# Four attention scalings moved from GpSimd to ScalarE, and the first weight unit cast by two engines

## The chip, the cores and the metric

The kernel runs on one core of a Trainium2 chip. One core has five engines that work side by side, each through its own list of instructions in a fixed order: TensorE (PE: matrix products, and transposes against an identity), VectorE (DVE), ScalarE (ACT), GpSimd (POOL) and SyncE (SP), which here issues nearly all of the transfers (DMAs). An instruction starts when the one ahead of it on its engine has gone and when the semaphores that it waits for have come. The working memory is SBUF; matrix products are written to PSUM, which has eight banks of 128 x 512 float32. The metric is the time of one execution in device microseconds; lower is better.

## The reference

One decoder layer on 512 tokens of 2048 channels, in float32. The normed input goes through one projection whose columns feed three mixers; their outputs go through one output projection, a residual, a second norm and a SwiGLU.

```python
h = _rms_norm(x, norm1_g[l])
proj = h @ w_in[l]
aq, ak, av, bu, bg, cq, ck, cv = jnp.split(proj, splits, axis=-1)
...
out_a = _dilated_mixture(aq, ak, av)              # 8 heads x 64
out_b = _conformer_conv(bu, bg, ...)              # 512 channels, 31 taps
out_c, _ = _band_attention(cq, ck, cv, 127, sinks=...)   # 16 query heads, 2 key heads
mix = jnp.concatenate([out_a, out_b, out_c], axis=-1)
x = x + mix @ w_out[l]
h2 = _rms_norm(x, norm2_g[l])
x = x + (jax.nn.silu(h2 @ w_gate[l]) * (h2 @ w_up[l])) @ w_down[l]
```

For one head of group A the three dilated patterns are one softmax over all earlier keys in which a key's weight is multiplied by the number of patterns that hold it (0 to 3). So a head needs scores, a masked maximum, exponentials, a product with that number, a sum, and a division by the sum before the values are weighed.

## The kernel before, in words

**Products in three terms.** A float32 product is made of three products of a rounded type: each operand is split into a high part `hi` (a cast, on ScalarE) and a low part `lo` (operand less high part, on VectorE), and `mm3` multiplies high by high, one high by the other low, and low by high. In the first stage the tokens are the operand loaded into the array and the weights the one that streams. All the kernel's rows of 128 x 512 on TensorE are such terms.

**Weights.** `pump` (L277 holds its transfer) loads weight units of up to 128 x 1024 in a fixed order into a few raw buffers. `split_up_to` (L289 the cast on ScalarE, L290 the subtraction on VectorE) makes `wh` and `wl` of a unit, two units ahead of the products that use it; there are three buffers of each.

**Opening.** For tile `k` of the 16 tiles of 128 channels, `scaled` makes the high part of the normed input on ScalarE (L419) and the low part on VectorE (L420). Then 12 products (four token tiles `in0` to `in3`, three terms each: L312, L313, L314) are added to four banks. The first two units hold the weights of one tile `k` each (128 x 512). Eight products of zeros (L409) run while the first data come in.

**Projection, attention, output projection.** Later units are taken one after the other (`project`, then `first_two` and a loop for the output projection `o`). Work of the mixers is hung between the products by a table of due times (`Ticks`): TensorE's order is written out by the main loop, and each `ticks.tick()` appends what is due to the lists of all engines. So where an instruction stands in an engine's list is fixed when the program is built, and an instruction that must wait holds up what stands behind it on its engine.

**One head of group A** (`attention`, name `a0` to `a3` for a pair of heads, head 0 or 1 in it). The four query tiles have 128, 256, 384 and 512 keys, in three units: `e..0` (tiles of 128 and 256), `e..1` (384), `e..2` (512: the last query tile). For each unit: `scores` on TensorE into a PSUM bank `s`; `top` on VectorE (L750, L753); `exps` on ScalarE (L763, out of PSUM into an SBUF tile `e`); `norm`: VectorE multiplies by the number of patterns and sums (L775), takes the reciprocal (L777), and GpSimd scales the tile by it (L779). Then `flip` transposes the tiles on TensorE (L795) into a bank `t`, ScalarE and VectorE split that bank (L801 `ph`, L806 `pl`), and `weigh` multiplies by the values (L819, L820) into a bank `o`, which L828 (ScalarE) and L833 (VectorE) put together in `mix`.

**Splitting the mixers' outputs.** `split_mix` casts a tile of the mixed outputs on ScalarE (L864, `mh`) and subtracts on GpSimd for group C or on VectorE for A and B (L865, `ml`). The output projection's first two column tiles (`first_two`) use `mh` and `ml` of rows c0, c1, c2, c4, c5, c3, c7, c6 in this order, six products a row, and they begin while heads `a1` to `a3` are still under way.

**Keys of the pair `a3`** pass over a bank too: `ak3wide` (L622, ScalarE), transposes (L629) into the bank `ak3t`, and two VectorE instructions that read it (L635). PSUM banks go round: the second transposes of head 1 of `a1` write the bank that `ak3t` had, and `aq3f` (L568) the one that the scores of 384 keys of `a2` had.

Of the kernel before, what the change touches and what calls it, by code (L numbers as in the profile page):

```python
# [9 lines left out]
F32 = mybir.dt.float32  # L10
F32R = mybir.dt.float32r
I32 = mybir.dt.int32
AF = mybir.ActivationFunctionType
ALU = mybir.AluOpType

P = 128
T = 512
NT = T // P
D = 2048
KT = D // P  # L20
# [67 lines left out]
C_G1, C_G2, C_CW, C_CB, C_LG, C_LB, C_QK, C_SINK, C_ALL = 0, 16, 32, 156, 160, 164, 168, 172, 188  # L88
# [34 lines left out]
def kernel(ctx: ExitStack, tc: tile.TileContext, xT, wi, wo, wgu, wd, cst_in, outT):  # L123
    nc = tc.nc
# [33 lines left out]
    units = [wi[0][:, :T], wi[0][:, T:]] + [wi[u] for u in range(1, 2 * N_IN)]  # L158
# [7 lines left out]
    raws, held = {}, {}  # L166
# [101 lines left out]
    splits = {}  # L268
# [11 lines left out]
    def split_up_to(i):  # L280
        while at["split"] <= min(i, len(works) - 1):
            key, last, eng = works[at["split"]]
            t, n = drop(key) if last else raws[key]
            u = at["split"]
            hi = wp.tile([P, 1024], F32R, name=f"wh{u}", tag="hi", bufs=SPLIT_BUFS)
            lo = wp.tile([P, 1024], F32R, name=f"wl{u}", tag="lo", bufs=SPLIT_BUFS)
            if eng or u < len(units) + 4:
                eng = eng or nc.vector
                nc.scalar.copy(hi[:, :n], t[:, :n])  # L289
                eng.tensor_sub(lo[:, :n], t[:, :n], hi[:, :n].bitcast(F32))  # L290
            else:
                near = psum["high"].tile([P, 1024], F32R, name=f"wn{u}", tag="h")
                nc.scalar.copy(near[:, :n], t[:, :n])
                nc.scalar.copy(hi[:, :n], t[:, :n])
                nc.vector.tensor_sub(lo[:, :n], t[:, :n], near[:, :n].bitcast(F32))  # L295
            splits[u] = (hi, lo)
            at["split"] += 1
# [13 lines left out]
    def mm3(out, wh, wl, xh, xl, start, stop):  # L311
        nc.tensor.matmul(out, wh, xh, start=start, stop=False)  # L312
        nc.tensor.matmul(out, wh, xl, start=False, stop=False)  # L313
        nc.tensor.matmul(out, wl, xh, start=False, stop=stop)  # L314
# [4 lines left out]
    xs = []  # L319
# [6 lines left out]
    for k in range(X_AHEAD):  # L326
        load_first(k)
        u = k if k < 2 else k // 2 + 1
# [18 lines left out]
    def col(i):  # L347
        return cst[:, i:i + 1]
# [64 lines left out]
    def scaled(x, g, tag, k):  # L413
        if k < N_WIDE:
            both = wide(k, f"{tag}{k}", F32R)
            hi, lo = both[:, :T], both[:, T:]
        else:
            hi, lo = slot(f"{tag}h{k}", F32R), slot(f"{tag}l{k}", F32R)
        nc.scalar.activation(hi, x, AF.Copy, scale=g)  # L419
        nc.vector.scalar_tensor_tensor(lo, x, g, hi.bitcast(F32), op0=ALU.mult, op1=ALU.subtract)  # L420
        return hi, lo
# [19 lines left out]

    g4 = [(column if j < COLUMN_BANKS - 1 else bank)(f"in{j}") for j in range(HEAD4)]
    h_hl = {}
    for k in range(2):
        h_hl[k] = scaled(xs[k], col(C_G1 + k), "h", k)
        split_up_to(k)
    pump(RAW_EARLY)
    add_square(ssum, xs[0], 0, "sq")
    for k in range(KT):
        if k + 2 < KT:  # L450
            h_hl[k + 2] = scaled(xs[k + 2], col(C_G1 + k + 2), "h", k + 2)
        if k < 2 or k % 2 == 0:
            wh, wl = next_unit()
            o = 0
        if k + X_AHEAD < KT:
            load_first(k + X_AHEAD)
        if k == 4:
            nc.sync.dma_start(cst[:, C_G2:], cst_in[:, C_G2:])
        if k + 1 < KT:
            add_square(ssum, xs[k + 1], k + 1, "sq")  # L460
        hi, lo = h_hl.pop(k)
        h_hi.append(hi)
        h_lo.append(lo)
        for i in range(NT):
            s = slice(i * P, (i + 1) * P)
            mm3(g4[i], hi[:, s], lo[:, s], wh[:, o:o + T], wl[:, o:o + T], k == 0, k == KT - 1)
        o += T
    xs = None
    c64 = cp.tile([P, NT], F32, name="c64")
# [245 lines left out]
    def attention(kind, box, mix, mi, heads):  # L715
        ready, every, step, s1, sx, s2, fl, ev, we = C_TICKS if kind == "c" else A_TICKS
        name = mi
# [5 lines left out]
        def head(h):  # L723
            es = {}
            d = cp.tile([P, 4, NT], F32, name=f"{name}d{h}", tag="soft", bufs=6)
            mx, nm, den, rd = (d[:, i] for i in range(4))
# [41 lines left out]
            def norm(u):  # L768
                e = es[u]
                s = slice(us[u][0][0], us[u][-1][0] + 1)  # L770
                if kind == "c":
                    nc.vector.tensor_add(den[:, s], den[:, s], mx[:, s])
                else:
                    for i, k0, n, o in us[u]:
                        nc.vector.scalar_tensor_tensor(e[:, o:o + n], e[:, o:o + n], 1.0, mult_a[:, T - n:],  # L775
                                                       op0=ALU.mult, op1=ALU.mult, accum_out=den[:, i:i + 1])
                nc.vector.reciprocal(rd[:, s], den[:, s])  # L777
                for i, k0, n, o in us[u]:
                    nc.gpsimd.tensor_scalar(e[:, o:o + n], e[:, o:o + n], rd[:, i:i + 1], None, op0=ALU.mult)  # L779

            ph, pl = {}, {}

# [57 lines left out]
            t0 = max(ticks.now + ready, head_at[0], box["q at"] - s1, box["k at"], box["v at"] - at_v)  # L840
# [37 lines left out]
    g4 = b = None  # L878
# [151 lines left out]
    for half in range(2):  # L1030
        for i, n in enumerate(OUT_ORDER[half]):
# [9 lines left out]
            wh, wl = next_unit()  # L1041
            if half == 1 and i == KT - 1:
                drop(first_sum[0][1])
            for kk in range(8):
                if half == 1 and i == KT - 2 and kk == 4:
                    first_sum[0][0]()
                k = 8 * half + kk
# [4 lines left out]
                s = slice(kk * P, (kk + 1) * P)  # L1052
# [345 lines left out]
    for g in range(2 * NP + N_DOWN):  # L1398
        t = g - 2 * NP
# [136 lines left out]
```

## Time and profile before

| | |
|---|---|
| median of 3 runs | 1879.7 us (1879.08 to 1879.79) |
| the profiled execution | 1879.36 us; its span, first to last instruction, 1877.5 us |
| TensorE clock granted | 1.000 |
| busy: PE, DVE, ACT, POOL | 1871.7, 1454.1, 1343.7, 1217.0 us |
| the chain of work that ended last | 96% PE, 1% each DVE, ACT, POOL and issue |
| 397 to 414 us: busy PE, DVE, ACT, POOL | 16.44, 15.50, 12.74, 16.19 of 17.00 us |

Rows of the timeline give start, duration, engine, line, operation and tiles, and in brackets how long the engine was idle just before and what ended that. Matrix products overlap: the duration of a row is longer than the step from its start to the next start, and a wait shows as a longer step. Vector and scalar instructions overlap too, by about a tenth of a microsecond. PEld is the load of the stationary operand, which runs ahead of its product.

### The profile page before, as it was taken

The page shows a single profiled execution, that of the slowest core. Times are in us where ns is not written, and L with a number is a line of the kernel's source. Part 1 is how long each engine was busy: PE and PEld are TensorE (multiplying, and loading weights), DVE is VectorE, ACT ScalarE, POOL GpSimd, SP SyncE. Part 2 cuts the span into 40 slices and gives each one's busy share as a digit, 9 for nine tenths or more (in the row PEclk, how much of TensorE's full clock was granted, in tenths as well). Part 3 has the DMA queues.
Part 4 walks back from the last instruction along what each step waited for, and adds up shares of the span by engine and source line. Part 5 has one row for each costly group of instructions (what it writes and reads, how often), then busy time and mean ns, then how long its engine had stood idle before and what let it go on. Part 6 is the DMA issues. An engine that isn't in the chain of part 4 may idle for free.

```text
span 1877.5 us, 28557 instructions
## 1 busy us (share of the span) xinstructions
PE 1871.7 (100%) x9848; PEld 1609.1 (86%) x9848; DVE 1454.1 (77%) x2376; ACT 1343.7 (72%) x1883; POOL 1217.0 (65%) x812
## 2 busy tenths in 40 slices
PE   9999999999999999999999999999999999999999
PEld 7888888888888888888888888888888888888888
DVE  7578999897679777777777777777777677778887
ACT  6246655553466887888878888888888887777675
POOL 5023444362155887778878877888787767766786
PEclk9999999999999999999999999999999999999999
DMA  7333233333342354443544445344455475578984
GB/s 271 122 109 102 81 105 102 121 107 138 113 146 89 114 178 142 163 163 132 184 134 164 162 137 181 132 166 160 145 175 196 151 237 185 196 253 283 311 241 124
DMA packets 157986, 301.09 MB, mean 160 GB/s; under 512 B 29968, under 2 KB 69008, under 8 KB 157840
## 3 DMA queue, kind: packets, MB, share of 16 engines
q1 hardware_dynamic: 157696, 299.25, 48.8%
q8 instruction: 78, 1.28, 0.3%
q14 instruction: 68, 0.56, 0.1%
q10 hardware_dynamic: 144, 0.01, 0.0%
HBM read 241.27 MB, written 50.33 MB: 155 GB/s over the span
## 4 chain that ended last, share of the span: by engine, by line
PE 96%; DVE 1%; issue 1%; ACT 1%; POOL 1%; DMA 0%; SPq 0%; DVEq 0%; POOLq 0%; ACTq 0%
PE out L1125 51%; PE out L1267 16%; PE o L313 3%; PE o L314 3%; PE o L312 3%; PE cq L312 1%; PE cq L313 1%; PE cq L314 1%; PE in L313 1%; PE ak L312 1%; PE bg L312 1%; PE ak L314 1%; PE ak L313 1%; PE bu L312 1%; PE bu L314 1%; PE bg L313 1%
## 5 line engine op out<-in xcount | busy, mean ns | idle before, releaser
L1125 PE MATMUL out<-h,wh 128*128 128x512 f32 x2464 | 588.4, 391 | 0.0
L1125 PEld LDWEIGHTS out<-h,wh 128*128 128x128 f32 x2464 | 452.7, 188 | 87.5
L1125 PEld LDWEIGHTS out<-h,wl 128*128 128x128 f32 x2464 | 316.2, 191 | 12.4 <-DVE wl L295 0.4
L1125 PE MATMUL out<-h,wl 128*128 128x256 f32 x2464 | 320.3, 283 | 0.2 <-DVE wl L295 0.2
L1267 PE MATMUL out<-wh,a 128*128 128x512 f32 x896 | 221.3, 389 | 0.0
L1267 PEld LDWEIGHTS out<-wh,a 128*128 128x128 f32 x896 | 168.2, 188 | 34.9
L289 ACT CAST wh<-w 128x1024 fp32r<-128x1024 f32 (+1 forms) x93 | 96.7, 1042 | 125.0 <-PE o L313 43.3
L290 DVE TENSOR_TENSOR wl<-w,wh 128x1024 fp32r<-128x1024 f32 (+1 forms) x93 | 117.2, 1262 | 46.7 <-ACT wh L289 45.7
L1267 PE MATMUL out<-wl,a 128*128 128x512 f32 x448 | 119.7, 389 | 0.0
L1267 PEld LDWEIGHTS out<-wl,a 128*128 128x128 f32 x448 | 84.1, 188 | 17.4
L513 DVE SCALAR_TENSOR_TENSOR y<-bu,cst,y 128x511 f32<-128x511 f32 (+14 forms) x120 | 90.3, 753 | 0.7
L1125 PE MATMUL out<-a,wh 128*128 128x512 f32 x330 | 80.1, 391 | 0.0
L1125 PEld LDWEIGHTS out<-a,wh 128*128 128x128 f32 x330 | 60.2, 188 | 11.4
L312 PE MATMUL o<-mh_c,wh 128*128 128x512 f32 x128 | 51.2, 400 | 0.0
L313 PE MATMUL o<-ml_c,wh 128*128 128x512 f32 x128 | 50.1, 392 | 0.4 <-POOL ml_c L865 0.3
L314 PE MATMUL o<-mh_c,wl 128*128 128x512 f32 x128 | 50.1, 391 | 0.0
L1312 DVE TENSOR_TENSOR Y<-Y,out 128x512 f32<-128x512 f32 x48 | 30.8, 683 | 19.0 <-PE out L1267 18.9
L1125 PEld LDWEIGHTS out<-a,wl 128*128 128x128 f32 x330 | 43.3, 191 | 2.2
L1125 PE MATMUL out<-a,wl 128*128 128x256 f32 x330 | 44.0, 283 | 0.0
L429 POOL TENSOR_TENSOR ssum<-ssum,sq 128x512 f32<-128x512 f32 x15 | 26.6, 1770 | 19.3 <-ACT sq L428 18.8
L312 PE MATMUL cq<-hh,wh 128*128 128x512 f32 x96 | 38.6, 402 | 0.0
L314 PE MATMUL cq<-hh,wl 128*128 128x512 f32 x96 | 37.5, 391 | 0.0
(3111 smaller groups left out, 5197.0 us busy)
## 6 DMA issues: line engine op xcount, KB each, us to landing
od<-a SPq DMA_DIRECT2D x140, 256.0 KB, 4.7
a<-od SPq DMA_DIRECT2D x140, 256.0 KB, 6.2
w<-in_wi SPq DMA_DIRECT2D x59, 512.0 KB, 3.6
w<-in_wo SPq DMA_DIRECT2D x32, 512.0 KB, 3.6
x<-in_xT SPq DMA_DIRECT2D x16, 256.0 KB, 6.7
xr<-in_xT SPq DMA_DIRECT2D x16, 256.0 KB, 3.8
x2d<-xr SPq DMA_DIRECT2D x16, 256.0 KB, 2.0
yd<-z SPq DMA_DIRECT2D x16, 256.0 KB, 5.5
```

The source lines that it names most:

```text
L289: nc.scalar.copy(hi[:, :n], t[:, :n])
L290: eng.tensor_sub(lo[:, :n], t[:, :n], hi[:, :n].bitcast(F32))
L312: nc.tensor.matmul(out, wh, xh, start=start, stop=False)
L313: nc.tensor.matmul(out, wh, xl, start=False, stop=False)
L314: nc.tensor.matmul(out, wl, xh, start=False, stop=stop)
L429: eng.tensor_add(acc, acc, sq)
L513: nc.vector.scalar_tensor_tensor(yconv[j][:, i:], hconv[j][:, :T - i], c, yconv[j][:, i:], op0=ALU.mult, op1=ALU.add)
L1125: nc.tensor.matmul(out, lhs[:, s], rhs, start=begin, stop=last and low == flip[0] and x is xs[-1], skip_group_check=True)
L1267: nc.tensor.matmul(to[h], x[:, h * P:(h + 1) * P], v[:, j], start=sub == 0 and h not in started, stop=sub == 1 and n in (len(todo) - 1, le ...
L1312: nc.vector.tensor_add(t, t, b)
```

## The change

There are two parts. They touch no transfer's order and no product's operands.

*Last query tiles of `a1` and `a2`.* In `norm`, the tile of 512 keys of both heads of `a1` and of `a2` is scaled by ScalarE (an activation that copies with a scale per partition) and no longer by GpSimd: four instructions. The order of the lists follows: the instruction now stands in ScalarE's list where GpSimd's stood in time.

*First weight unit.* VectorE casts the first 128 columns of unit 0 and ScalarE the other 384 (before: ScalarE all 512); the first tile's 12 products go term by term over the four token tiles: high x high four times, low tokens x high weights four times, high tokens x low weights four times.

```diff
+            if u == 0:
+                nc.vector.tensor_copy(hi[:, :P], t[:, :P])
+            elif eng or u < len(units) + 4:
...
-    for k in range(2):
-        h_hl[k] = scaled(xs[k], col(C_G1 + k), "h", k)
-        split_up_to(k)
+    t0 = raws[0][0]
+    split_up_to(0)
+    h_hl[0] = scaled(xs[0], col(C_G1), "h", 0)
+    hi, lo = splits[0]
+    nc.scalar.copy(hi[:, P:T], t0[:, P:T])
+    nc.vector.tensor_sub(lo[:, :T], t0[:, :T], hi[:, :T].bitcast(F32))
+    t0 = None
+    h_hl[1] = scaled(xs[1], col(C_G1 + 1), "h", 1)
+    split_up_to(1)
...
+        if k == 0:
+            for x, w in ((hi, wh), (lo, wh), (hi, wl)):
+                for i in range(NT):
+                    nc.tensor.matmul(g4[i], x[:, i * P:(i + 1) * P], w[:, :T], start=x is hi and w is wh, stop=False)
+            continue
...
-                    nc.gpsimd.tensor_scalar(e[:, o:o + n], e[:, o:o + n], rd[:, i:i + 1], None, op0=ALU.mult)
+                    if name in ("a1", "a2") and i == 3:
+                        nc.scalar.activation(e[:, o:o + n], e[:, o:o + n], AF.Copy, scale=rd[:, i:i + 1])
+                    else:
+                        nc.gpsimd.tensor_scalar(e[:, o:o + n], e[:, o:o + n], rd[:, i:i + 1], None, op0=ALU.mult)
```

TensorE's list at the opening, first tile, before. `in0` to `in3` are the four banks, `wh0` and `wl0` the halves of unit 0; the tile named `h0` holds both the high and the low part of the input (L314 reads the low one).

```order
L312 MATMUL in0_139<-wh0_146,h0_143 128x512
L313 MATMUL in0_139<-wl0_147,h0_143 128x512
L314 MATMUL in0_139<-wh0_146,h0_143 128x512
L312 MATMUL in1_140<-wh0_146,h0_143 128x512
L313 MATMUL in1_140<-wl0_147,h0_143 128x512
L314 MATMUL in1_140<-wh0_146,h0_143 128x512
L312 MATMUL in2_141<-wh0_146,h0_143 128x512
L313 MATMUL in2_141<-wl0_147,h0_143 128x512
```

The same place on TensorE in the changed kernel, the first nine:

```order
L475 MATMUL in0_139<-wh0_143,h0_146 128x512
L475 MATMUL in1_140<-wh0_143,h0_146 128x512
L475 MATMUL in2_141<-wh0_143,h0_146 128x512
L475 MATMUL in3_142<-wh0_143,h0_146 128x512
L475 MATMUL in0_139<-wh0_143,h0_146 128x512
L475 MATMUL in1_140<-wh0_143,h0_146 128x512
L475 MATMUL in2_141<-wh0_143,h0_146 128x512
L475 MATMUL in3_142<-wh0_143,h0_146 128x512
L475 MATMUL in0_139<-wl0_144,h0_146 128x512
```

The first product that reads `wl0` stood second and stands ninth. The second tile's products are in the old order in both.

ScalarE's list where head 1 of `a1` ends, before. `a1e12` is the tile of 512 keys of head 1, `wh63` the high half of a weight unit, `mh_c2` and `mh_c4` high parts of rows c2 and c4.

```order
L763 ACTIVATE a1e12_4064<-a1s12_3975,a1d1_3612,aq1r_3746 128x512
L801 CAST a1ph02_4069<-a1t02_4036 128x256
L563 COPY aq3raw_4089<-aq3_3938 128x512
L289 CAST wh63_4119<-w63_3545 128x1024
L864 CAST mh_c2_4126<-mix_c2_2446 128x512
L622 COPY ak3wide_4138<-ak3r_4073 128x512
L864 CAST mh_c4_4140<-mix_c4_3088 128x512
L763 ACTIVATE a2e00_4159<-a2s00_4042,a2d0_3780,aq2r_3921 128x128
```

The same place on ScalarE in the changed kernel (lines are moved by 13 to 16):

```order
L776 ACTIVATE a1e12_4065<-a1s12_3976,a1d1_3613,aq1r_3747 128x512
L817 CAST a1ph02_4070<-a1t02_4037 128x256
L793 ACTIVATE a1e12_4065<-a1e12_4065,a1d1_3613 128x512
L576 COPY aq3raw_4090<-aq3_3939 128x512
L291 CAST wh63_4120<-w63_3546 128x1024
L880 CAST mh_c2_4127<-mix_c2_2447 128x512
L635 COPY ak3wide_4139<-ak3r_4074 128x512
L880 CAST mh_c4_4141<-mix_c4_3089 128x512
```

The new row L793 stands ahead of the copy, the weight cast and the casts of the mixed rows; all else keeps its order.

GpSimd's list at the same place, before and then changed; `ml_c2`, `ml_c4` and `ml_c5` are low parts of mixed rows.

```order
L585 TENSOR_TENSOR ak3r_4073<-ak3v_4055,nhalf_106 128x8
L779 TENSOR_SCALAR a1e12_4064<-a1e12_4064,a1d1_3612 128x512
L865 TENSOR_TENSOR ml_c2_4127<-mix_c2_2446,mh_c2_4126 128x512
L865 TENSOR_TENSOR ml_c4_4141<-mix_c4_3088,mh_c4_4140 128x512
L865 TENSOR_TENSOR ml_c5_4173<-mix_c5_2209,mh_c5_4172 128x512
```

And GpSimd in the changed kernel:

```order
L598 TENSOR_TENSOR ak3r_4074<-ak3v_4056,nhalf_106 128x8
L881 TENSOR_TENSOR ml_c2_4128<-mix_c2_2447,mh_c2_4127 128x512
L881 TENSOR_TENSOR ml_c4_4142<-mix_c4_3089,mh_c4_4141 128x512
L881 TENSOR_TENSOR ml_c5_4174<-mix_c5_2210,mh_c5_4173 128x512
L795 TENSOR_SCALAR a2e00_4160<-a2e00_4160,a2d0_3781 128x128
```

The scaling of `a1e12` is gone from this list, so that `ml_c2` follows `ak3r` directly.

More of the change, by code (lines that the diff above doesn't have):

```diff
@@ L286, in split_up_to @@
             lo = wp.tile([P, 1024], F32R, name=f"wl{u}", tag="lo", bufs=SPLIT_BUFS)
-            if eng or u < len(units) + 4:
+            if u == 0:
+                nc.vector.tensor_copy(hi[:, :P], t[:, :P])
+            elif eng or u < len(units) + 4:
                 eng = eng or nc.vector
@@ L463 @@
         h_lo.append(lo)
+        if k == 0:
[3 more added lines that the diff above has]
+            continue
         for i in range(NT):
             s = slice(i * P, (i + 1) * P)
-            mm3(g4[i], hi[:, s], lo[:, s], wh[:, o:o + T], wl[:, o:o + T], k == 0, k == KT - 1)
+            mm3(g4[i], hi[:, s], lo[:, s], wh[:, o:o + T], wl[:, o:o + T], False, k == KT - 1)
         o += T
```

## The prediction

> **What bounds the kernel now.** The page comes first: in the table, TensorE is busy 1871.7 us of a span of 1877.5 us, and the chain that ended last is 96% TensorE. So only what TensorE waits for can be won, and only what newly makes it wait can be lost. I read next who TensorE's loads of the stationary operand waited for over the whole span (total us, times, longest). These are the rows that the change can touch:
>
> ```profile
> PEld o L313 <- POOL ml_c L865: 1.1, 2, 0.7
> PEld in L313 <- DVE wl L290: 1.1, 3, 0.5
> ...
> PEld a1t L795 <- PE o L314: 0.5, 1, 0.5
> ```
>
> The first row is low parts that come late from GpSimd, the second low halves of weights in the opening, the third transposes of head 1 of `a1`. The row names TensorE itself for the third; of the transposes' two conditions (their bank read out, and the product before them), the bank is meant, as shown below. Together they are 2.7 us, 0.14% of the time, and a load's wait is partly covered by the product before it. I therefore take the losses from TensorE's own steps, from start to start. The step of undisturbed products is 405.95 - 405.73 = 0.22 to 0.23 us in the second set of rows below.
>
> **The opening.** The timeline, TensorE, ScalarE and VectorE in turn:
>
> ```profile
> 5.26 0.50 PE L312 MATMUL in<-wh,h 128*128 128x512 f32 x1
> 5.99 0.50 PE L313 MATMUL in<-wl,h 128*128 128x512 f32 x1 [0.23 <-DVE wl L290]
> ...
> 8.88 0.47 PE L313 MATMUL in<-wl,h 128*128 128x512 f32 x1
> ...
> 11.76 0.50 PE L313 MATMUL in<-wl,h 128*128 128x512 f32 x1
> ...
> 4.59 0.62 ACT L289 CAST wh<-w 128x512 fp32r<-128x512 f32 x1
> 6.67 0.73 ACT L419 ACTIVATE h<-x,cst 128x512 fp32r<-128x512 f32 x1 [1.46 <-DMA x<-in_xT]
> 7.45 0.62 ACT L289 CAST wh<-w 128x512 fp32r<-128x512 f32 x1
> ...
> 9.40 1.05 ACT L289 CAST wh<-w 128x1024 fp32r<-128x1024 f32 x1 [0.18 <-DMA w<-in_wi]
> ...
> 5.24 0.69 DVE L290 TENSOR_TENSOR wl<-w,wh 128x512 fp32r<-128x512 f32 x1
> ...
> 8.11 0.69 DVE L290 TENSOR_TENSOR wl<-w,wh 128x512 fp32r<-128x512 f32 x1
> ...
> 10.48 1.22 DVE L290 TENSOR_TENSOR wl<-w,wh 128x1024 fp32r<-128x1024 f32 x1 [0.48 <-ACT wh L289]
> ```
>
> The second product stands 0.73 us behind the first where 0.23 would do: 0.50 us lost to `wl0` (5.24 + 0.69 = 5.93). In the changed kernel ScalarE casts 384 of the 512 columns, 0.62 x 3/4 = 0.47 us (0.62 if length did not matter), so the first product starts 0 to 0.15 us earlier, at 5.11 to 5.26. VectorE's cast of 128 columns has no row; a quarter of the 0.69 of L290 is 0.17, and the whole 0.69 bounds it (nothing at the other end). It moves `wl0` to 6.1, at worst 6.6. That is needed only by the ninth product, at 5.11 + 8 x 0.23 = 6.95, so the cast is hidden. The first tile's twelve products then end at about 7.9 to 8.0, some 0.7 us earlier than before.
>
> That does not last. The second product of the next tile reads `wl1`, which VectorE ends at 8.11 + 0.69 = 8.80, from ScalarE's cast at 7.45, which stands behind the activation at 6.67, which waited for a transfer of x. None of these moves. So this product starts at 8.88 as before, and the 0.7 us become idle time ahead of it. The next tile has the same end: `wl2` is there at 10.48 + 1.22 = 11.70, its cast at 9.40 waited for a transfer, and its product starts at 11.76 as before. The opening's term is 0, with -0.1 to +0.1 for edges. If the cover is gone (x and weights landing 0.7 us earlier) it would be -0.5.
>
> **Three losses at 402 to 413 us.** TensorE's rows:
>
> ```profile
> 402.46 0.47 PE L312 MATMUL o<-mh_c,wh 128*128 128x512 f32 x1
> 403.07 0.50 PE L313 MATMUL o<-ml_c,wh 128*128 128x512 f32 x1
> ...
> 405.73 0.39 PE L313 MATMUL o<-ml_c,wh 128*128 128x512 f32 x1
> 405.95 0.39 PE L314 MATMUL o<-mh_c,wl 128*128 128x512 f32 x1
> 406.48 0.63 PE L795 MATMUL a1t<-ident,a1e 128*128 128x128 f32 x4
> ...
> 412.56 0.40 PE L312 MATMUL o<-mh_c,wh 128*128 128x512 f32 x1
> 413.25 0.50 PE L313 MATMUL o<-ml_c,wh 128*128 128x512 f32 x1 [0.28 <-POOL ml_c L865]
> ```
>
> L313 at 403.07 and at 413.25 read `ml` tiles: (0.61 - 0.23) + (0.69 - 0.23) = 0.38 + 0.46 us lost. The transposes at 406.48 follow by 0.53 instead of 0.23: 0.30 us. The sum, 1.14 us, is all that freeing GpSimd can give back. Now the other engines at that place:
>
> ```profile
> 397.50 0.59 ACT L563 COPY aq3raw<-aq 128x512 f32<-128x512 f32 x1 [2.68 <-PE aq L314]
> 397.98 1.05 ACT L289 CAST wh<-w 128x1024 fp32r<-128x1024 f32 x1
> 398.93 0.62 ACT L864 CAST mh_c<-mix_c 128x512 fp32r<-128x512 f32 x1
> ...
> 400.49 0.91 ACT L763 ACTIVATE a2e<-a2s,a2d,aq2r 128x128 f32<-128x128 f32 x2
> ...
> 407.14 0.59 ACT L801 CAST a1ph<-a1t 128x512 fp32r<-128x512 f32 x1 [1.04 <-PE a1t L795]
> ...
> 398.68 0.16 DVE L777 RECIPROCAL a1d<-a1d 128x1 f32<-128x1 f32 x1
> ...
> 399.08 1.22 DVE L290 TENSOR_TENSOR wl<-w,wh 128x1024 fp32r<-128x1024 f32 x1
> ...
> 400.87 0.16 DVE L753 SCALAR_TENSOR_TENSOR a2d<-a2d,aq2r 128x1 f32<-128x1 f32 x1
> ...
> 403.10 1.19 DVE L753 SCALAR_TENSOR_TENSOR a2d<-a2d,aq2r 128x1 f32<-128x1 f32 x1
> ...
> 404.81 1.52 DVE L635 SCALAR_TENSOR_TENSOR ak<-ak3raw,gqk,ak3t 64x512 f32<-64x512 f32 x2
> ...
> 399.04 2.62 POOL L779 TENSOR_SCALAR a1e<-a1e,a1d 128x512 f32<-128x512 f32 x1
> 401.63 4.43 POOL L865 TENSOR_TENSOR ml_c<-mix_c,mh_c 128x512 fp32r<-128x512 f32 x3
> ```
>
> *What GpSimd's row removes.* The scaling of head 1's last tile, 2.62 us at 399.04, stands ahead of three `ml` at 401.63. Without it GpSimd would be free for `ml_c2` at 399.04.
>
> *What ScalarE's row adds.* The new instruction stands ahead of the copy at 397.50, but it needs the reciprocal, which VectorE ends at 398.68 + 0.16 = 398.84. ScalarE, in order, must wait until about 398.88. The instruction's own price: same form as L419 (copy with a scale per partition, 512 columns), 0.73 us at 6.67; a row overlaps its follower by 0.59 - 0.48 = 0.11, so 0.62 of the engine. (Ends: 0.5, a plain copy's step, and 0.73.) The copy starts at 399.50 instead of 397.50, and all behind it is 2.0 us later until ScalarE's next idle time, 1.04 us at 407.14.
>
> *First loss.* `mh_c2` moves from 398.93 to 400.93 and ends, with its 0.62, at 401.55. `ml_c2` on GpSimd can start then: at 401.63, where it started before. GpSimd's list is free earlier, but its input comes exactly so much later. The 0.38 us stay: term 0, -0.1 to +0.1.
>
> *Second loss.* VectorE's `wl63` at 399.08 now waits for ScalarE's cast, 397.98 + 2.0 + 1.05 = 401.03: 1.95 us late. What stands behind it on VectorE (the maximum and the products of `a2`, fed by exponentials that slip from 400.49 to 402.5, then the pair L635 at 404.81) slips by some 1.75 us (0.2 us allowed for the gaps between its rows). L635 reads the bank `ak3t` and ended at 404.81 + 1.52 = 406.33; the load for the transposes into that bank followed at once, their row at 406.48. So TensorE waits for VectorE here. How late L635 is now hangs on one row: L753 at 403.10 took 1.19 us for one column, though the same form took 0.16 at 400.87. It ended just when a GpSimd `ml` did (three in 4.43 us from 401.63, the second to about 404.4). If it runs free this time, VectorE gets 1.03 of the 1.75 back and TensorE's wait grows by 0.7; if the third `ml` holds it (404.85 to about 405.8), by 1.65.
>
> The Trainium skill, "SBUF — State Buffer", section "Who interferes with whom", says that a VectorE instruction with two SBUF inputs and a GpSimd one that reads SBUF exclude each other for the whole instruction, and that who issues second waits. The row of 1.19 us agrees; the one of 0.16 us ran while GpSimd's scaling was under way, and does not. By that rule the sum would be at its upper end, by the row of 0.16 at its lower one.
>
> *Third loss.* GpSimd starts its `ml` row at 401.63 as before and does the same work after it, so the last `ml` is still there at about 413.2. TensorE, 0.7 to 1.65 us late, comes after that: the 0.46 us are no longer lost. Net at 413 us: 0.7 - 0.46 = +0.24 to 1.65 - 0.46 = +1.19. I take the middle, +0.7, since neither of the two L753 rows is nearer.
>
> *The other three moved scalings* fall where ScalarE idled:
>
> ```profile
> 389.76 1.05 ACT L289 CAST wh<-w 128x1024 fp32r<-128x1024 f32 x1 [3.68 <-PE aq L313]
> ...
> 413.78 2.00 ACT L289 CAST wh<-w 128x1024 fp32r<-128x1024 f32 x2 [2.54 <-PE o L313]
> ...
> 434.29 1.05 ACT L289 CAST wh<-w 128x1024 fp32r<-128x1024 f32 x1 [4.18 <-PE o L313]
> ...
> 387.49 1.91 POOL L779 TENSOR_SCALAR a1e<-a1e,a1d 128x512 f32<-128x512 f32 x1 [1.77 <-PE aq L313]
> ...
> 414.80 2.37 POOL L779 TENSOR_SCALAR a2e<-a2e,a2d 128x512 f32<-128x512 f32 x1 [1.60 <-DVE a2d L777]
> ...
> 434.76 1.57 POOL L779 TENSOR_SCALAR a2e<-a2e,a2d 128x512 f32<-128x512 f32 x1 [5.01 <-DVE a2d L777]
> ```
>
> Head 0 of `a1`: the reciprocal is there by 387.49; with 0.62 and the two exponentials now behind it (0.91 at 400.49) ScalarE is done by 389.1, before its next row at 389.76. Head 0 of `a2`: ready by 414.80, so the weight casts of 413.78 slip by 414.80 + 0.62 - 413.78 = 1.6. Head 1: 434.76 + 0.62 - 434.29 = 1.1. Those casts are for units two ahead, and a unit is 24 products x 0.23 = 5.5 us of TensorE, which hides both; without that cover they would cost 1.6 + 1.1. GpSimd's 1.91, 2.37 and 1.57 us there come back as idle time. TensorE does not wait again in this stage, so what it is late at 413 us it carries to the end.
>
> **Sum.** Against the profiled execution: 1879.36 + 0 (opening) + 0.7 = 1880.1. The median of the three runs lies 0.34 us above that execution, so I say 1880.2, between 1880.1 and 1879.7 + 0.7.
>
> **The rivals.** A: GpSimd's relief gets through. If the reciprocal came some 2 us earlier, ScalarE would not wait, `ml_c2` would start by 400 and the three losses go: 1879.36 - 1.14 = 1878.2, and 1877.7 if the opening's 0.5 is kept too. For it: GpSimd is 16.19 of 17.00 us busy there (table) and holds VectorE up at least once. Against it: the reciprocal's row stands behind VectorE work that the change leaves alone.
>
> B: the opposite side, one mechanism: ScalarE's wait is passed on in full. It decides at the pair L635. If it ends later than about 406.8, the change costs time; to be over 0.2% slower it must end at 410.5 or later (3.8 + 0.46 us). The terms at hand, 1.95 with no slack taken, two `ml` holds of 1.4 and 1.0, give 406.33 + 4.3 = 410.7 and the time 1879.36 + 4.3 - 0.46 = 1883.2. No single row speaks for so much.
>
> C: the opening does what it says and no more comes of the rest: 1879.36 - 0.5 = 1878.9. The transfers at 6.67 and 9.40 speak against it.
>
> **How the numbers follow.** Forecast (+0.2 to +1.2) 0.62; A 0.22; C 0.10; B 0.04; something not seen, faster by over 0.2%, 0.02. About 0.2%, 3.8 us, is what a measurement of this kernel can tell from no change; the forecast, A and C all lie inside. So faster 0.02, same 0.93, slower 0.05 (B, and a little of the forecast's tail). The forecast alone spans 1879.5 to 1880.9 with the offset of the median. The range takes in A's near end and some way towards B: 1878.0 to 1881.5.
>
> **What would show it.** Opening: first product near 5.1, twelve steps of 0.23 without a hole, then a hole ahead of the product of `wl1`, still at about 8.9, and that of `wl2` at 11.8. Attention: ScalarE idle ahead of the new row until about 398.9, the copy near 399.5, `wl63` near 401.0, `ml_c2` near 401.6, the transposes after L635 at 407.2 to 408.2, no hole ahead of the last `ml`. The prediction is wrong if TensorE reaches 414 us earlier than before, or if a new wait of over 1 us stands anywhere after 440 us.

## The result, and the profile after

The changed kernel takes 1882.09 us (median of 20 runs, 1881.56 to 1882.57) against 1879.44 us before (20 runs, 1878.83 to 1879.91): ratio 1.0014, 95% interval 1.0008 to 1.002. It is 2.65 us slower, and the whole interval lies above 1. That is under the 0.2% that the forecast named as its bound for "the same", but the time lies above the forecast range of 1878.0 to 1881.5. The granted clock is 1.00, as before. The profiled execution took 1882.12 us. In the experiments below a few executions of most kernels, of the kernel before too, took 1.3 to 2.2 us longer than the others at the same clock, so that the highest times stand far from the medians.

Its page, first the span and the totals, then the chain that ended last:

```profile
span 1880.3 us, 28551 instructions
...
PE 1872.0 (100%) x9848; PEld 1609.1 (86%) x9848; DVE 1457.1 (77%) x2377; ACT 1345.6 (72%) x1887; POOL 1209.0 (64%) x808
...
PE 96%; DVE 3%; ACT 1%; issue 0%; DMA 0%; SPq 0%; DVEq 0%
```

TensorE's work is the same (1871.7 us before); the span is 2.8 us longer, so the loss is idle time. What TensorE waited for in the changed kernel (total us, times, longest):

```profile
PE a1t L811 <- DVE ak L648: 1.7, 1, 1.7
...
PE a1t L811 <- DVE mix_a L849: 1.1, 1, 1.1
PE o L315 <- POOL ml_c L881: 0.5, 1, 0.5
```

Two waits are new: the second and the third transposes of head 1 of `a1` (L811, L795 before) wait for VectorE, 1.7 us for the pair that reads the bank `ak3t` (L648, L635 before) and 1.1 us for `mix_a` (L849, L833 before). The busy times of the stretch that the table of before shows (PE, PEld, DVE, ACT and POOL, each with its count):

```profile
397.00:414.00 17.00, 13.76 (x72) 10.83 (x71) 14.68 (x33) 13.12 (x25) 12.66 (x11) 1.00 0.43 114
```

GpSimd is 3.5 us less busy there (16.19 before), 2.62 us of it by the scaling that has left its list, and TensorE does 2.7 us less in the same stretch (16.44 before). The rows of the stretch, ScalarE, VectorE, GpSimd and TensorE in turn:

```profile
398.89 0.72 ACT L793 ACTIVATE a1e<-a1e,a1d 128x512 f32<-128x512 f32 x1 [4.12 <-DVE a1d L790]
399.52 0.57 ACT L576 COPY aq3raw<-aq 128x512 f32<-128x512 f32 x1
399.98 1.05 ACT L291 CAST wh<-w 128x1024 fp32r<-128x1024 f32 x1
400.94 0.61 ACT L880 CAST mh_c<-mix_c 128x512 fp32r<-128x512 f32 x1
...
401.06 1.23 DVE L292 TENSOR_TENSOR wl<-w,wh 128x1024 fp32r<-128x1024 f32 x1 [1.89 <-ACT wh L291]
...
403.58 1.51 DVE L788 SCALAR_TENSOR_TENSOR a2e<-a2e,mult_a 128x256 f32<-128x256 f32 x1
...
405.98 0.27 DVE L766 SCALAR_TENSOR_TENSOR a2d<-a2d,aq2r 128x1 f32<-128x1 f32 x1
...
406.78 1.52 DVE L648 SCALAR_TENSOR_TENSOR ak<-ak3raw,gqk,ak3t 64x512 f32<-64x512 f32 x2
408.33 2.87 DVE L687 TENSOR_TENSOR av<-av3s,av 128x256 fp32r<-128x256 f32 x2
411.23 0.68 DVE L849 TENSOR_TENSOR mix_a<-mix_a,a1o 64x512 f32<-64x512 f32 x1
...
401.63 4.61 POOL L881 TENSOR_TENSOR ml_c<-mix_c,mh_c 128x512 fp32r<-128x512 f32 x3 [2.57 <-ACT mh_c L880]
406.22 2.02 POOL L795 TENSOR_SCALAR a2e<-a2e,a2d 128x128 f32<-128x128 f32 x2
408.20 2.71 POOL L881 TENSOR_TENSOR ml_c<-mix_c,mh_c 128x512 fp32r<-128x512 f32 x2
...
402.53 0.47 PE L314 MATMUL o<-mh_c,wh 128*128 128x512 f32 x1
403.48 0.50 PE L315 MATMUL o<-ml_c,wh 128*128 128x512 f32 x1 [0.47 <-POOL ml_c L881]
...
406.34 0.40 PE L316 MATMUL o<-mh_c,wl 128*128 128x512 f32 x1
408.44 0.63 PE L811 MATMUL a1t<-ident,a1e 128*128 128x128 f32 x4 [1.71 <-DVE ak L648]
...
410.51 0.40 PE L316 MATMUL o<-mh_c,wl 128*128 128x512 f32 x1
411.96 0.44 PE L811 MATMUL a1t<-ident,a1e 128*128 128x128 f32 x2 [1.06 <-DVE mix_a L849]
...
415.77 0.40 PE L314 MATMUL o<-mh_c,wh 128*128 128x512 f32 x1
416.00 0.39 PE L315 MATMUL o<-ml_c,wh 128*128 128x512 f32 x1
```

And the rows of the kernel before that answer to them and that the prediction did not show:

```profile
401.44 0.43 DVE L775 SCALAR_TENSOR_TENSOR a2e<-a2e,mult_a 128x256 f32<-128x256 f32 x1 [0.16 <-ACT a2e L763]
...
406.36 0.76 DVE L674 TENSOR_TENSOR av<-av3s,av 128x256 fp32r<-128x256 f32 x2
407.15 0.68 DVE L833 TENSOR_TENSOR mix_a<-mix_a,a1o 64x512 f32<-64x512 f32 x1
...
406.05 1.79 POOL L779 TENSOR_SCALAR a2e<-a2e,a2d 128x128 f32<-128x128 f32 x2
407.80 2.92 POOL L865 TENSOR_TENSOR ml_c<-mix_c,mh_c 128x512 fp32r<-128x512 f32 x2
...
408.54 0.39 PE L314 MATMUL o<-mh_c,wl 128*128 128x512 f32 x1
408.77 0.38 PE L795 MATMUL a1t<-ident,a1e 128*128 128x128 f32 x2
```

Read the two sets side by side. ScalarE's copy is 2.02 us later (397.50 to 399.52), and VectorE's list from `wl63` on with it (399.08 to 401.06): the `av` pair, two subtractions that make the low part of a3's values, goes from 406.36 to 408.33. GpSimd's list hardly moves: its two `ml` (rows c3 and c7) go from 407.80 to 408.20. Before, the pair ran beside GpSimd's two scalings and took 0.76 us. Now it starts just behind GpSimd's `ml`, takes 2.87 us, and ends 0.3 us behind them (411.2 and 410.9). `mix_a` behind it is there 4.08 us later.

TensorE's losses, below called its holes, each a step less the 0.23 us of an undisturbed one:

| at | before | after | difference |
|---|---|---|---|
| `ml_c2` | 0.38 | 403.48 - 402.53 - 0.23 = 0.72 | +0.34 |
| transposes after `ak3t` | 0.30 | 408.44 - 406.34 - 0.23 = 1.87 | +1.57 |
| transposes after `mix_a` | 408.77 - 408.54 - 0.23 = 0 | 411.96 - 410.51 - 0.23 = 1.22 | +1.22 |
| last `ml` | 0.46 | 416.00 - 415.77 - 0.23 = 0 | -0.46 |

The sum is +2.67 us. TensorE came 0.07 us later to the first of them (402.46 before, 402.53 now), and the last product stands 416.00 - 413.25 = 2.75 us later. The medians differ by 2.65.

The opening, TensorE, ScalarE and VectorE:

```profile
5.37 2.40 PE L475 MATMUL in<-wh,h 128*128 128x512 f32 x8
...
8.91 0.50 PE L315 MATMUL in<-wl,h 128*128 128x512 f32 x1
...
11.80 0.41 PE L315 MATMUL in<-wl,h 128*128 128x512 f32 x1
...
4.80 0.51 ACT L450 CAST wh<-w 128x384 fp32r<-128x384 f32 x1 [0.44 <-DMA w<-in_wi]
...
4.80 0.23 DVE L288 CAST wh<-w 128x128 fp32r<-128x128 f32 x1 [3.15 <-DMA w<-in_wi]
```

The products of `wl1` and `wl2` start at 8.91 and 11.80 (8.88 and 11.76 before), whatever the first tile does. And the first tile itself gains little: the product behind its twelve starts at 8.51 against 8.66 before, since the weights came late and the first two steps took 0.60 and 0.28 us (products at 5.37, 5.96 and 6.24). Why these steps are that long, no run shows.

### The profile page after: what moved, and what is told of

Same layout as the page of the kernel before. It is cut to its first block, busy times and chain, and to the rows that moved or that the text cites. A ratio compares the mean times of both kernels' runs of the same rounds, so it can differ in the third digit from the quotient of the medians.

```text
span 1880.3 us, 28551 instructions
## 1 busy us (share of the span) xinstructions
PE 1872.0 (100%) x9848; PEld 1609.1 (86%) x9848; DVE 1457.1 (77%) x2377; ACT 1345.6 (72%) x1887; POOL 1209.0 (64%) x808
## 4 chain that ended last, share of the span: by engine, by line
PE 96%; DVE 3%; ACT 1%; issue 0%; DMA 0%; SPq 0%; DVEq 0%
PE out L1141 51%; PE out L1283 16%; PE o L314 3%; PE o L315 3%; PE o L316 3%; PE cq L314 1%; PE cq L315 1%; PE cq L316 1%; PE ak L314 1%; PE bg L314 1%; PE ak L316 1%; PE ak L315 1%; PE bu L316 1%; PE bu L314 1%; PE bg L315 1%; PE bg L316 1%
## 5 line engine op out<-in xcount | busy, mean ns | idle before, releaser
L314 PE MATMUL o<-mh_c,wh 128*128 128x512 f32 x128 | 51.3, 401 | 0.0
L314 PE MATMUL cq<-hh,wh 128*128 128x512 f32 x96 | 38.6, 402 | 0.0
```

## The experiments

Each kernel was timed beside the kernel before on one chip. The ratio is that of the mean times, so it can differ a little from that of the medians. The 95% intervals of these ratios reach about 0.09% to either side, 1.7 us; where a difference is smaller than that, its verdict rests on the rows of the trace. For this the last column has the sum of TensorE's holes from 402 to 416 us in the profiled execution, less the 1.14 us (0.38, 0.30 and 0.46) of the kernel before. It leaves out what an execution wins or loses elsewhere: the profiled ones differ by up to 0.6 us before they come to this place. The whole change has +2.67 us there. All times in one table, then one by one:

| run | us, median of 11 (lowest to highest) | before | difference | ratio (95%) | holes |
|---|---|---|---|---|---|
| opening alone | 1879.52 (1879.1 to 1880.92) | 1879.61 | -0.09 | 0.9998 (0.9989 to 1.0007) | +0.03 |
| head 1 of `a1` alone | 1882.01 (1881.62 to 1882.42) | 1879.61 | +2.40 | 1.0012 (1.0003 to 1.0021) | +2.67 |
| other three scalings | 1879.52 (1879.3 to 1879.77) | 1879.61 | -0.09 | 0.9997 (0.9988 to 1.0006) | 0.00 |
| the wait alone | 1881.77 (1881.26 to 1883.74) | 1879.61 | +2.16 | 1.0012 (1.0003 to 1.0021) | +2.24 |
| scaling left out | 1879.93 (1879.78 to 1880.3) | 1879.43 | +0.50 | 1.0003 (0.9994 to 1.0012) | +0.79 |
| scaling one tick late | 1880.54 (1879.88 to 1882.47) | 1879.43 | +1.11 | 1.0007 (0.9999 to 1.0016) | +1.01 |
| changed, without `ml` c3, c7 | 1880.70 (1880.07 to 1882.49) | 1879.43 | +1.27 | 1.0007 (0.9998 to 1.0016) | +1.44 |
| before, without `ml` c3, c7 | 1878.69 (1878.3 to 1880.86) | 1879.43 | -0.74 | 0.9997 (0.9988 to 1.0006) | -0.46 |
| before, `av` pair moved | 1879.12 (1878.54 to 1880.94) | 1879.48 | -0.36 | 0.9999 (0.999 to 1.0008) | -0.46 |
| changed, `av` pair moved | 1880.57 (1880.2 to 1882.41) | 1879.48 | +1.09 | 1.0007 (0.9998 to 1.0016) | +1.45 |
| one tick late, `av` pair moved | 1879.34 (1878.92 to 1881.22) | 1879.48 | -0.14 | 1.0002 (0.9993 to 1.001) | -0.22 |

### Which part of the change it is

Three runs take the change apart. The opening alone:

```diff
-    for k in range(2):
-        h_hl[k] = scaled(xs[k], col(C_G1 + k), "h", k)
-        split_up_to(k)
...
+            for x, w in ((hi, wh), (lo, wh), (hi, wl)):
+                for i in range(NT):
+                    nc.tensor.matmul(g4[i], x[:, i * P:(i + 1) * P], w[:, :T], start=x is hi and w is wh, stop=False)
```

> The kernel before with the opening's part of the change alone (no attention scaling moved). By the wait theory (all of the loss comes from the one scaling of a1's head 1, whose instruction on ScalarE waits for VectorE's reciprocal) the time is that of before within 0.2 us: the second tile's products keep their starts near 8.9 and 11.8 us. A rival, that part of the 2.65 us is the opening's, gives 0.3 to 1 us more than before; the saving of 0.5 us that the opening was made for would give 1878.9.

One scaling alone, and the other three without it:

```diff
-                    nc.gpsimd.tensor_scalar(e[:, o:o + n], e[:, o:o + n], rd[:, i:i + 1], None, op0=ALU.mult)
+                    if name == "a1" and h == 1 and i == 3:
+                        nc.scalar.activation(e[:, o:o + n], e[:, o:o + n], AF.Copy, scale=rd[:, i:i + 1])
+                    else:
+                        nc.gpsimd.tensor_scalar(e[:, o:o + n], e[:, o:o + n], rd[:, i:i + 1], None, op0=ALU.mult)
```

> The kernel before with one scaling moved to ScalarE: the last query tile of head 1 of a1. Wait theory: all of the loss, +2.4 to +2.9 us over before, with the copy of aq3 on ScalarE near 399.5 and transposes of a1 held to about 408.4 and 412.0 us. Rival (the four scalings each cost some of it): 0.6 to 1.5 us.

```diff
-                    nc.gpsimd.tensor_scalar(e[:, o:o + n], e[:, o:o + n], rd[:, i:i + 1], None, op0=ALU.mult)
+                    if i == 3 and (name == "a2" or (name == "a1" and h == 0)):
+                        nc.scalar.activation(e[:, o:o + n], e[:, o:o + n], AF.Copy, scale=rd[:, i:i + 1])
+                    else:
+                        nc.gpsimd.tensor_scalar(e[:, o:o + n], e[:, o:o + n], rd[:, i:i + 1], None, op0=ALU.mult)
```

> The kernel before with the other three scalings moved: head 0 of a1 and both heads of a2. Wait theory: nothing, -0.2 to +0.2 us, though ScalarE waits about 2 us for the reciprocal at head 0 of a1 too, because no row of ScalarE behind that place is due soon. Rival (each moved scaling costs): +1 to +2 us.

Measured: -0.09, +2.40 and -0.09 us. The single scaling has the same two new waits as the whole change (1.7 and 1.1 us), the same holes and the same span, 1880.3 us. With the opening alone the first product starts at 5.02 us, and those of `wl1` and `wl2` at 8.91 and 11.77, as in the whole change. So the loss belongs to one instruction of the four; the opening and the other three scalings cost and bring nothing that shows.

### The wait without the relief, and the relief without the wait

Here GpSimd keeps the scaling, and ScalarE gets a copy of one column of the reciprocal at the place where the change puts its scaling:

```diff
+                    if name == "a1" and h == 1 and i == 3:
+                        nc.scalar.copy(small("after"+name, 1), rd[:, i:i + 1])
```

> The kernel before, GpSimd's scalings all kept, with one instruction added to ScalarE at the place of the new one for head 1 of a1: a copy of the reciprocal, one column. ScalarE gets the wait (until about 398.9 us) without the 0.6 us of work, and GpSimd gets no relief. Wait theory: +1.5 to +2.7 us over before (ScalarE 1.5 us late instead of 2.0). Rival (the loss comes from the scaling's own time on ScalarE, or from GpSimd's rows that start together later): 0 to +0.3 us.

Measured +2.16 us, with the same two waits of TensorE. Its rows:

```profile
399.11 0.19 ACT L780 COPY aftera<-a1d 128x1 f32<-128x1 f32 x1 [4.07 <-DVE a1d L777]
399.21 0.58 ACT L563 COPY aq3raw<-aq 128x512 f32<-128x512 f32 x1
...
408.04 2.87 DVE L674 TENSOR_TENSOR av<-av3s,av 128x256 fp32r<-128x256 f32 x2
...
399.27 1.58 POOL L781 TENSOR_SCALAR a1e<-a1e,a1d 128x512 f32<-128x512 f32 x1
```

The scaling's own work on ScalarE is not what costs: 0.19 us of work with the wait ahead of it does nearly the whole damage. GpSimd's scaling takes 1.58 us here and 2.62 before, where VectorE's subtraction of `wl63` ran beside it.

The counterpart: the tile is scaled by no engine (its rows stay un-normalised), so GpSimd is relieved and ScalarE waits for nothing:

```diff
-                    nc.gpsimd.tensor_scalar(e[:, o:o + n], e[:, o:o + n], rd[:, i:i + 1], None, op0=ALU.mult)
+                    if not (name == "a1" and h == 1 and i == 3):
+                        nc.gpsimd.tensor_scalar(e[:, o:o + n], e[:, o:o + n], rd[:, i:i + 1], None, op0=ALU.mult)
```

> The kernel before without the scaling of the last query tile of head 1 of a1 on any engine (left out, so those 128 rows are not normalised). GpSimd gets the relief and ScalarE no wait. Relief theory: ml of row c2 starts at about 399.6 instead of 401.63 us, and the holes ahead of the products of ml (0.38 and 0.46 us) close; the hole at the transposes (0.30) stays or grows a little, since VectorE sets it: -0.5 to -0.9 us against before. Rival (VectorE's holds by GpSimd move with GpSimd's rows and eat it): 0 to -0.3 us.

Measured +0.50 us, above both expected ranges, though the interval holds them too; TensorE's holes, +0.79 us, leave no gain. VectorE and GpSimd in that run, and then what TensorE waited for:

```profile
401.31 1.50 DVE L775 SCALAR_TENSOR_TENSOR a2e<-a2e,mult_a 128x256 f32<-128x256 f32 x1
...
406.06 2.87 DVE L674 TENSOR_TENSOR av<-av3s,av 128x256 fp32r<-128x256 f32 x2
...
399.35 4.62 POOL L866 TENSOR_TENSOR ml_c<-mix_c,mh_c 128x512 fp32r<-128x512 f32 x3 [0.59 <-ACT mh_c L865]
...
405.94 2.71 POOL L866 TENSOR_TENSOR ml_c<-mix_c,mh_c 128x512 fp32r<-128x512 f32 x2
```

```profile
PE a1t L796 <- DVE mix_a L834: 1.1, 1, 1.1
PE a1t L796 <- DVE ak L635: 0.5, 1, 0.5
```

GpSimd starts its `ml` row 2.28 us earlier than before (401.63), 0.29 us of it because this execution is ahead by that much all along, and the waits for `ml` are gone from TensorE. The first of them, 0.38 us, brings nothing even so: VectorE's readers of `ak3t` have not moved, so TensorE only waits longer at the next place, 0.70 us in place of 0.30. And GpSimd's two `ml` of c3 and c7 move from 407.80 to 405.94, and now meet the `av` pair, which has stayed where it was. What the change does by moving VectorE back, this does by moving GpSimd forward. The first theory, that the relief is worth half a microsecond or more by itself, falls.

### The scaling on ScalarE, without its wait

The scaling is issued one tick later, behind the copy, the weight cast, `mh_c2` and `ak3wide`, so that the reciprocal is there:

```diff
+                    if name == "a1" and h == 1 and i == 3:
+                        ticks.after(1, lambda e=e[:, o:o + n], r=rd[:, i:i + 1]: nc.scalar.activation(e, e, AF.Copy, scale=r))
...
```

> The kernel before with the scaling of head 1 of a1 on ScalarE, issued one due time later, so that it stands in ScalarE's list behind the copy of aq3, the weight cast, the cast of row c2 and the wide copy of ak3. The reciprocal is there by then (398.84 us), so ScalarE pays 0.6 us and waits for nothing. Wait theory: the loss is gone, -0.9 to 0 us against before. Rival (the loss is the work moved to ScalarE while it is nearly full, 12.7 of 17 us): +1 us or more.

Measured +1.11 us, where a gain or nothing was expected. That is the rival's number; that its reason, the work on ScalarE, is not the cause is shown further down, where the same work stays and the loss goes. ScalarE's copy is back at 397.50, but the pair is held as in the run without the scaling:

```profile
401.60 1.26 DVE L775 SCALAR_TENSOR_TENSOR a2e<-a2e,mult_a 128x128 f32<-128x128 f32 x1
...
406.57 2.88 DVE L674 TENSOR_TENSOR av<-av3s,av 128x256 fp32r<-128x256 f32 x2
...
406.45 2.71 POOL L868 TENSOR_TENSOR ml_c<-mix_c,mh_c 128x512 fp32r<-128x512 f32 x2
```

So the meeting of VectorE and GpSimd at the `av` pair costs time by itself, without a wait of ScalarE. In the changed kernel it is ScalarE's wait that brings it about, by moving VectorE back; here and in the run before this one GpSimd comes early instead.

### Is it GpSimd that holds the pair?

The `ml` of rows c3 and c7 are left out (the high part stands in for the low one), in the changed kernel and, as a control, in the kernel before:

```diff
-            (nc.gpsimd if name[0] == "c" else nc.vector).tensor_sub(lo, m, hi.bitcast(F32))
+            if name not in ("c3", "c7"):
+                (nc.gpsimd if name[0] == "c" else nc.vector).tensor_sub(lo, m, hi.bitcast(F32))
+            else:
+                lo = hi
```

> The changed kernel without GpSimd's subtractions for rows c3 and c7 (left out; the high part is used in place of the low one). In the changed kernel these two ran from 408.20 to 410.91 us, while VectorE's pair for the values of a3 took 2.87 us instead of 0.76. Hold theory (a GpSimd instruction with two inputs keeps VectorE waiting): the pair takes 0.76 us again, the third transposes of head 1 do not wait for mix_a, and of the changed kernel's loss 1.0 to 1.4 us go: 1880.7 to 1881.1. Rival (the pair waits for something else, the cast of av3 or a transfer): 1882.1 as before, the pair still over 2 us.

> The control: the kernel before without the same two subtractions. Here they ran from 407.80 to 410.72 us and kept GpSimd from the last row c6, whose product had a hole of 0.46 us. Expected -0.3 to -0.5 us against before, from that hole. If it gains as much as the changed kernel does, the hold is no part of the change's loss.

Measured: +1.27 us and -0.74 us. In the changed kernel without these two, the pair is short again although it starts where it did (this execution is 0.28 us ahead all along), and TensorE's wait for `mix_a` is gone:

```profile
408.04 0.76 DVE L687 TENSOR_TENSOR av<-av3s,av 128x256 fp32r<-128x256 f32 x2
```

That shows GpSimd's two subtractions to be what stretches the pair from 0.76 to 2.87 us. The single rows of the changed kernel fit: the first of the pair ends at 409.75 us, 0.28 behind the first `ml` (409.47), and the second at 411.2, as far behind the second (410.9). What the hold costs is read from TensorE's holes. The changed kernel without the two has 1.44 us in place of 2.67, 1.23 less, and that is the hole ahead of the transposes that wait for `mix_a`. In the kernel before, where the pair is not held, only the hole ahead of the last `ml` goes, 0.46 us, as expected; the changed kernel has not got that one any more. So the control does not gain what the changed kernel gains. (The medians say 1.38 us, 2.65 less 1.27, and 0.74; these too are smaller than the intervals.)

### The pair taken out of the way

Nothing needs the low parts of a3's values before 485 us. So the pair can be written two ticks later, behind `mix_a` in VectorE's list, with all work kept:

```diff
-            ticks.after(1, low)
+            ticks.after(3 if name == "av3" else 1, low)
```

In the kernel before, in the changed one, and in the one with the scaling a tick late:

> The kernel before, with VectorE's pair of av3 (L674, which makes the low part of a3's values) written two ticks later, behind mix_a; nothing of a3 needs it before about 485 us. Theory (the hold by GpSimd's two-input rows is one half of the change's loss and the wait of ScalarE the other): in the kernel before, the pair takes 0.76 us and stands unheld, so moving it alone is worth little: -0.5 to +0.3 us against the kernel before. Rival (the pair is late for the transposes even unheld): -0.8 us or more.

> The changed kernel with the same move. The 2.87 us of the held pair would stand behind mix_a and not ahead of it. Theory: the wait of TensorE for mix_a (1.06 us) goes and the wait for ak3t (1.7 us) stays: -1.0 to -1.4 us against the changed kernel, 1880.7 to 1881.1. Rival (GpSimd's rows hold whatever of VectorE stands there, so mix_a or the next operation is held in place of the pair): within 0.4 us of the changed kernel.

> The kernel before with the scaling of a1e12 on ScalarE one tick later (as in the run with the late scaling) and the pair of av3 moved. Theory: with ScalarE's wait gone and the held pair off the path of the transposes, the rest is the hold ahead of ak3t (0.8 us): 1879.0 to 1879.8, that is -0.5 to +0.3 against the kernel before. Rival (late scaling loses by something else than the held pair): +0.8 to +1.3, as without the move.

Measured: -0.36, +1.09 and -0.14 us, against 0, +2.65 and +1.11 with the pair in its old place. The first and the last are inside what was expected; the second, 1880.57 us, is 0.1 us under it. The changed kernel with the pair moved, what TensorE waited for:

```profile
PE a1t L811 <- DVE ak L648: 1.7, 1, 1.7
```

and VectorE's rows there:

```profile
407.75 0.68 DVE L849 TENSOR_TENSOR mix_a<-mix_a,a1o 64x512 f32<-64x512 f32 x1
408.35 0.95 DVE L788 SCALAR_TENSOR_TENSOR a2e<-a2e,mult_a 128x384 f32<-128x384 f32 x1
...
412.89 0.74 DVE L687 TENSOR_TENSOR av<-av3s,av 128x256 fp32r<-128x256 f32 x2
```

The wait for `mix_a` is gone and the wait for `ak3t` stays, as expected. By TensorE's holes the move is worth 2.67 - 1.45 = 1.22 us in the changed kernel, the same hole as in the table of steps, and the same that leaving out GpSimd's two rows closes. In the kernel before it is worth 0.46 us for another reason: the hole ahead of the last `ml` closes. (The medians say 1.56 and 0.36 us.) The rival (something else is held in its place) holds only in small: the 384-column product takes 0.95 us where it took 0.54, and nobody waits for it.

With the scaling late and the pair moved the loss is gone, so the work on ScalarE was not its cause. But no gain comes in its stead, for TensorE still waits for `ak3t`:

```profile
PE a1t L798 <- DVE ak L635: 0.8, 1, 0.8
```

The hole ahead of `ml_c2` has closed, so TensorE comes to this place 0.42 us earlier, and VectorE's L635 is 0.21 us later than before (both less the 0.29 us by which this execution is late all along). What is won at the first place is waited for at the next, as in the run without the scaling. No kernel of the study is faster than the one before by more than the intervals tell.

## Why the prediction was wrong, point by point

**Opening, 0.** The term is right, and so is what sets it: the next product that needs a low half starts at 8.91, and the one after at 11.80. Weights landed 0.2 us later in this execution, so the first product is at 5.37 and not near 5.1 (it is at 5.02 in the run of the opening alone); from the start of the cast to that product it is 0.57 us against 0.67. The sign "twelve steps of 0.23 without a hole" did not come: the first two steps are longer, the tile ends 0.15 us earlier than before and not 0.7, and the hole ahead of the product of `wl1` is 8.91 - 8.51 - 0.23 = 0.17 us. So even had x and the weights come earlier, there was no 0.5 us to keep: the tile's gain is 0.15 us here and 0.19 in the run of the opening alone.

**ScalarE's wait, 2.0 us.** Right to a tenth: the copy at 399.52 (forecast 399.5), `wl63` on VectorE at 401.06 (401.0), `ml_c2` on GpSimd at 401.63 (401.6).

**First loss, term 0.** Mis-sized: +0.34, and 0.07 before it. `ml_c2` starts where forecast, but takes 1.80 us where it took 1.39: the product that needs it is at 403.48. VectorE's subtraction of `wl63`, moved to 401.06 to 402.29, now lies beside it; no run takes that away, so this cause is argued. It does not add to the total, since TensorE would have waited for `ak3t` so much longer.

**Second loss, L635 0.7 to 1.65 us later, middle.** Mis-sized: L635 is 1.97 us later (404.81 to 406.78), above the upper bound, and the transposes 1.96 (406.48 to 408.44). The one-column row at 403.10, on which the choice hung, was indeed nearly free this time (0.27 us at 405.98), but the hold fell on the row of 256 columns ahead of it instead, 1.51 us at 403.58 for what took 0.43 before. Asking which of two rows would be held was the wrong question: GpSimd's three `ml` take 4.6 us, and in every run above in which the two lists had shifted against each other, some VectorE row beside them was stretched (1.26 to 1.51 us), as one was before (1.19). So nothing was given back, and the slip of `wl63`, 1.98 us, came through whole.

**Third loss, -0.46.** Right: the product of the last `ml` follows by 0.23 us, an undisturbed step.

**The step that failed** is the one that adds up "Net at 413 us" from 0.7 to 1.65 less 0.46. It lets VectorE's slip act on TensorE at one place only, the bank `ak3t`. VectorE's list is in order and stays late behind L635: the `av` pair, slipped by 1.97 us, ran into GpSimd's two `ml` and was held to 2.87 us, and `mix_a` behind it is what the third transposes wait for. That wait, 1.22 us, was in no term and no bound; without it the time would have been about 1880.9 us, inside the range (with the pair moved it was 1880.57). The prediction's own slip was enough to see it coming: 406.36 + 1.75 = 408.11 us for the pair, behind GpSimd's `ml` at 407.80. The rest is the size of the second loss: 1.96 where the middle of 0.7 and 1.65 was taken, 0.79 more. With the terms as measured the prediction's own sum is 1879.36 + 1.96 + 1.22 - 0.46 = 1882.08, against 1882.12 for the profiled execution and 1882.09 for the median. (The 0.34 us between that execution and the median, of which the forecast took a part, was an accident of three runs; with twenty it is 0.08.)

**The other three scalings, 0.** Right: 0.00 in TensorE's holes.

**Rivals.** A (the relief gets through) is refuted twice: ScalarE waits as forecast, and the relief alone (scaling left out) brings nothing. B, given a chance of 0.04, had the right mechanism, the wait passed on with GpSimd's holds on top, but put 4.3 us of it at `ak3t`; it was 1.96 there and 1.22 at the third transposes, 2.7 us net of the 0.46 where B had 3.8. C (the opening's 0.5) is refuted by the rows of the run with the opening alone; its median alone, -0.09 us, could not do it.

The Trainium skill, "SBUF — State Buffer", "Who interferes with whom", says that the order of issue decides which of the two engines blocks, and that the lock is for a whole instruction. The pair's 2.87 us when it starts just behind GpSimd's `ml` (408.33 and 408.20) agrees. So does L635 in the kernel before, one of whose two large inputs lies in PSUM (the rule, as the prediction quotes it, is for two in SBUF): at 404.81 it ran beside the last of three `ml` and took 1.52 us, no more than beside scalings in the changed kernel. The pair's 0.76 us in the kernel before does not: it started at 406.36, when GpSimd had begun a scaling of an SBUF tile at 406.05, and the measurement decides: the hold is shown for GpSimd's subtractions, not for its scalings. The prediction applied the rule to one row of VectorE; applied to the whole list behind that row, with GpSimd's list beside it, it points at the third transposes.

## What to carry to other kernels

Moving an operation to an emptier engine puts its wait into that engine's list: compare the time at which its operand is ready with the time at which the next instruction there used to start. That difference (1.4 us here) and the instruction's own step (0.6) are what everything behind it pays, and a copy of 0.19 us did nearly as much harm as the scaling of 0.72. Then follow the slip through every engine that reads from that list, and past the first place where it bites, up to the next idle time. Time won at one wait is worth nothing if another engine, which has not moved, sets the next one. Where two engines hold each other up, a slip of one against the other, in either direction, can break an alignment that cost nothing before; an instruction whose result is needed much later can be moved out of such a place.

## What the runs showed of the hardware that was not expected

Work taken from GpSimd made the kernel no faster, though GpSimd was 16.19 of 17.00 us busy and TensorE waited for it at two places: with the scaling gone altogether the time was no shorter (+0.50 us, and TensorE's holes 0.79 us longer). GpSimd's subtractions of two SBUF tiles go with VectorE rows stretched by factors of 3.8 (0.76 to 2.87 us, shown by leaving them out) and 3.5 (0.43 to 1.51, not tried). GpSimd's scalings of one SBUF tile did not stretch the pair at 406.36 or the one-column row at 400.87 (0.16 us); beside VectorE's subtraction of `wl63` it was the scaling that took longer (2.62 us against 1.58 without it).
